# An encoder trunk in float32 on one core: earlier norms, tables loaded under the output product, a weight limit of six, values one step later

## The chip, the cores and the metric

The kernel runs on one core of a Trainium2 chip. A core has five engines that take their instructions in order, each from its own queue: TensorE (PE, matrix products), VectorE (DVE), ScalarE (ACT), GpSimd (POOL) and SyncE (SP, which here only issues transfers). Transfers (DMAs) run beside them; the kernel issues them from SP, POOL and ACT. The metric is the time of one execution on the device in microseconds (us); lower is better.

## The reference

Two layers act on `x` (512 tokens, 1024 wide); each also reads 256 memory tokens. All is float32.

```python
for i in range(DEPTH):                       # 2
    h = rmsnorm(x, norm_g[i])
    mem_h = rmsnorm(mem, mem_norm_g[i])
    if i % 2 == 0:                           # layer 0: 8 heads x 3 dilation groups
        proj = einsum('bsd,de->bse', h, w_in_a[j])
        o_mix = mixer_dilated(qkv, qn_a[j], kn_a[j], ang_a)
    else:                                    # layer 1: 8 query heads, 2 key/value heads
        proj = einsum('bsd,de->bse', h, w_in_b[j])
        o_mix = mixer_axial_gqa(q, k, v, qn_b[j], kn_b[j], ang_b)
    o_mem = memory_attention(q_mem, mem_h, w_mem_kv[i], ...)      # 4 heads
    y = concatenate([o_mix, o_mem]) * silu(gate)
    x = x + einsum('bse,ed->bsd', y, w_out[i])
```

## The kernel before

**Products.** A float32 product is made of three products of a rounded type: every operand is split into a high half (a cast on ACT) and a low half (the difference, on DVE), and PE adds high x high, high x low and low x high (`mm3`, lines 163 to 166). For weights the cast is line 287 (tile `wh`) and the difference line 297 (tile `wo`).

**Blocks.** Most projections take seven quarter products instead of eight (Strassen's scheme as Winograd wrote it; `s_chunk`). A block is such a group of seven. Their left sides are sums and differences of quarters of the activations (`S1` to `S4`), their right sides the weight quarters "21", "11", "22" and the sums T1 to T4, which are formed by accumulating transfers: for layer 1's blocks T1 by line 252, T2 by 261, T3 by 266, T4 by 271, all issued on POOL. T2 is added from the finished T1, T4 from the finished T2. In `s_chunk` a PSUM bank is copied out by ACT (`keep`, line 364, tile `sn`) before a later product adds to the same bank.

**Order.** The program is written out slot by slot. After each unit of matmuls (some 24 small or 12 large ones) the code calls `drv.free()`, then `W.advance()`, which moves the weights one step, then `drv.tick()`, which runs one step of every waiting generator: the `urgent` ones, then the `bulk` ones (attention), then what was handed to `drv.late`. A `yield n` in a generator means: go on n slots later. What is issued in a tick stands in the engines' queues behind what came earlier in the code, and in order.

**Weights.** `W.dma` (line 229) loads pieces of 512 KB into a ring of 23 tiles of 4 KB a partition (`m4`), as long as the number of loaded pieces not yet split is below `KEEP` of the next piece's kind: T2b are the memory weights of layer 1, O1 the pieces of the output product that go without the seven-product scheme, W1b the seven blocks of layer 1's input projection that have one unit a product. `W.sum` issues the accumulating transfers two steps after the load; `W.hi` and `W.lo` do the two halves, up to four pieces ahead.

**The start.** `mem_kv` makes the memory's keys and values of layer 0; between its units `ahead` finishes the memory's norm (`norm_2`, `norm_3`) and `prep` (spawned for slot 2) norms x in four blocks: `norm_1` (two squares on ACT with their sums, then POOL), `norm_2` (two products on DVE, line 469), then transposes and splits (`first_t`, `diffs_t`, `rest_t`).

**Layer 0's end.** `attn_a` handles a head in some twenty steps. `scale` multiplies the exponentials by `c`, eight instructions on DVE (line 1157). `gates` multiplies the heads by the gate; in the last gate block (g is 2) the product (line 781), its cast on ACT (784) and the low half (786) stand in three steps. `out_proj` then makes the output product: one seven-product block, and `out_rest`, two plain products of four slots each. Behind it in the code come the rotary tables of layer 1: three loads (lines 1254 to 1259) and five DVE instructions (`setup_b`, lines 1262 to 1265).

**Layer 1's attention.** `attn_b` is a pipeline of 32 items (8 heads, 4 blocks of 128 queries). In one bulk step it scores item t, takes the exponentials of t-1, scales t-2, transposes t-3 (`turn`, line 1388; halves in `hi`, `lo`, lines 1392 and 1397) and multiplies t-4 by the values (`pv`, into tile `ob`). Every second `pv` makes a half of a head; a full head goes to memory (`odb`) and is loaded back by the gate (`og`, line 763).

Of the kernel before, what the change touches and what calls it, by code (L numbers as in the profile page):

```python
# [10 lines left out]
F32 = mybir.dt.float32  # L11
# [10 lines left out]
TCKW = {}  # L22
NBIG, NM4, NS2, SCRATCH = 7, 23, 13, 2048
RING, LEAD = 4, 2
BULK, ACTIVE, SET_AT, WARM, MEM_B, PREP_Y, ACC_AT, PREP_B, HALF, SET_B = 2, 2, 15, 1, 12, 1, 4, 1, {"a": 3, "b": 3, "o": 0}, 1
MEM_STEP = 1, 1
MEM_D = 4
PD = 2
# [7 lines left out]

SEQ = [1, 2, 0] + list(range(3, len(PLAN)))
T1_DMA = 17
KEEP = {"T2": 8, "T2b": 4, "O1": 4, "W1": 9, "W2": 10, "W2s": 9, "W1b": 7, "W2b": 9}


class Driver:
# [83 lines left out]
def trunk_kernel(ctx: ExitStack, tc: tile.TileContext, x, mem, wall, norm_g, mem_norm_g, gcol,  # L126
# [408 lines left out]
    def rest_t(H, c, ds):  # L535

        def put(k, f):
            hi, lo = slot(H, k, c)
            A.copy(hi, f)
            drv.late(lambda: V.tensor_tensor(lo, f, hi.bitcast(F32), ALU.subtract))  # L540

        cs = slice(c * 128, (c + 1) * 128)
        s1, s2_, s4, s3, f22 = [full[k][:, :, cs] for k in ("S1", "11", "12", "S3", "22")]
        V.tensor_tensor(s2_, s1, s2_, ALU.subtract)
        V.tensor_tensor(s4, s4, s2_, ALU.add)
        put("S2", s2_)
        yield ds[0]
        put("S4", s4)
        yield ds[1]
        put("S3", s3)  # L550
        yield ds[2]
        put("22", f22)
        yield 1
# [193 lines left out]
    def gates(od, o_done):  # L747
# [3 lines left out]
        def gate(H, first, g, half=False):  # L751


            yt = [[m4(F32R, "y").rearrange("p (h t) -> p h t", h=2) for _ in range(2)] for _ in range(2)] if g == 2 else None
            if g < 2:
                yf[g] = [m4(name="yf") for _ in range(2)]

            def ev(q, u, t):
                i, j = int(q[0]) - 1, int(q[1]) - 1
                h0, ts = first + 2 * j, slice(i * 256, (i + 1) * 256)  # L760
                def load():
                    o = s2(name="og")
                    nc.sync.dma_start(o.rearrange("p (h t) -> p h t", h=2), od[h0:h0 + 2, :, ts].rearrange("h p t -> p h t"))
# [17 lines left out]
                V.tensor_tensor(t, t, o, ALU.mult)  # L781
                yield 1
                tv = t.rearrange("p (h t) -> p h t", h=2)
                A.copy(yt[j][0][:, :, ts], tv)
                yield 1
                V.tensor_tensor(yt[j][1][:, :, ts], tv, yt[j][0][:, :, ts].bitcast(F32), ALU.subtract)
# [54 lines left out]

        return gate, prep_y, YW, ys

    def out_proj(YW, ys, src, evac, tiles, half=False):

        acc, done = {}, set()

# [14 lines left out]

        drv.spawn(load(), ACC_AT)
        s_chunk(512, YW, ev, half=half)
        out_rest(ys, acc, done, evac)


# [22 lines left out]
        if c % 2:  # L890
            W.dma(2)
    H, H2 = {}, {}
    xb = [halves(t) for t in xt]

    def prep():

        n = {}
        for c in range(5):
            if c < 4:
                n[c] = norm_1(xb[c])  # L900
            if c:
# [156 lines left out]
    def attn_a(h, qk0, qs, ks, v12, n_done):  # L1058
# [95 lines left out]
        def scale(o):  # L1154
            for b in range(4):
                c0, c1 = (64 if o == 0 and b == 0 else 0), (192 if o == 0 and b == 3 else 256)
                V.tensor_scalar(prob[o][:, b, c0:c1], prob[o][:, b, c0:c1], c[:, o, b:b + 1], 0.5, ALU.mult, ALU.mult)

        def turn(o):

# [85 lines left out]
                yield EO[2]  # L1246
                yield from rest_t(H2, b - 2, EO[3:])

    drv.spawn(mem_norm(1), MEM_B)
    out_proj(YW, ys, xv, ev_o, lambda: [m4(name="acc") for _ in range(2)])  # L1250

    ropeB = pool.tile([128, 2048], F32, tag="tabs", name="tabs", bufs=1).rearrange("p (a c b e) -> p a c b e", a=2, c=2, b=4)
    tb_raw = s2(name="tbraw").rearrange("p (c b e) -> p c b e", c=2, b=4)
    nc.sync.dma_start(tb_raw, tab_b.rearrange("p (c b e) -> p c b e", c=2, b=4))
    grB = s2(name="grB")[:, 0:256].rearrange("p (a e) -> p a e", a=2)
    nc.sync.dma_start(grB[:, 0], qn_b.to_broadcast([128, 128]))
    nc.sync.dma_start(grB[:, 1], kn_b.to_broadcast([128, 128]))

    def setup_b():
        V.tensor_scalar(grB[:, 0], grB[:, 0], QS, None, ALU.mult)
        for qk in range(2):
            for cs_ in range(2):
                V.tensor_tensor(ropeB[:, qk, cs_].rearrange("p b (h e) -> p b h e", h=2),
                                tb_raw[:, cs_, :, None, :].to_broadcast([128, 4, 2, 64]),
                                grB[:, qk].rearrange("p (h e) -> p h e", h=2)[:, None].to_broadcast([128, 4, 2, 64]), ALU.mult)
# [45 lines left out]
    def rope_b(t, qk, i, d):  # L1313
# [5 lines left out]
        V.tensor_tensor(v(ta), v(t), ropeB[:, qk, 0, 2 * i:2 * i + 2, None, :].to_broadcast([128, 2, 2, 128]), ALU.mult)  # L1319
        V.tensor_tensor(v(sb), v(t), ropeB[:, qk, 1, 2 * i:2 * i + 2, None, :].to_broadcast([128, 2, 2, 128]), ALU.mult)  # L1320
# [35 lines left out]
    def attn_b():  # L1356
# [51 lines left out]
        def out_(i):  # L1408
# [147 lines left out]
```

## Time and profile before

| | us |
|---|---|
| median of 3 runs | 972.17 |
| lowest, highest | 968.25, 972.54 |
| profiled execution, its own time | 966.39 |
| its span, first to last instruction | 964.6 |
| PE busy | 947.5 (98%) |
| DVE busy | 790.6 (82%) |
| ACT busy | 683.0 (71%) |
| POOL busy | 339.7 (35%) |
| granted TensorE clock, mean | 0.998 |

The profile is one execution, told by hardware. "L297" is line 297 of the kernel. A wait reads "who line <- who released it: us in total, times, longest". A row of a timeline has start, length, engine, line, operation, output<-inputs, size and count, and in brackets the idle time before it and what ended it. A window has busy time per engine, the granted clock, the share of the 16 DMA engines and GB/s. PEld is the loading of PE's fixed operand, which overlaps the matmuls.

### The profile page before, as it was taken

What the parts mean: (1) busy time and instruction counts of PE and PEld (TensorE: products, weight loads), DVE (VectorE), ACT (ScalarE), POOL (GpSimd) and SP (SyncE); (2) the same over time, 40 slices, a digit from 0 to 9 for tenths busy, and PEclk for the clock granted to TensorE, in tenths of its full rate; (3) what the DMA queues carried; (4) which work ended last, traced back from release to release, by engine and by line L of the source; (5) the groups of instructions that cost most, each with busy time, mean ns of one, the idle gap of its engine ahead of it and who ended that gap; (6) DMA issues with size and microseconds to landing.
All of it is one profiled execution on the core that took longest, in us unless ns stands there. A gap on an engine that the chain in (4) does not pass through costs nothing.

```text
span 964.6 us, 16613 instructions
## 1 busy us (share of the span) xinstructions
PE 947.5 (98%) x5682; PEld 833.3 (86%) x5682; DVE 790.6 (82%) x1411; ACT 683.0 (71%) x1701; POOL 339.7 (35%) x482
## 2 busy tenths in 40 slices
PE   8999999999999999999999999999899999999998
PEld 5879888888888888888899997888899999998876
DVE  4898676888888888888797999879888997779873
ACT  5874689686868686868675767556778887878760
POOL 1512523556454545464726011323233231011011
PEclk9999999999999999999999999999999999999999
DMA  9799946869686868685858989969976696877744
GB/s 361 234 285 341 288 112 177 288 123 265 147 259 151 258 155 261 154 262 132 269 147 216 276 194 281 310 198 308 284 174 148 175 239 163 222 202 173 191 144 131
DMA packets 89130, 209.81 MB, mean 218 GB/s; under 512 B 25299, under 2 KB 36051, under 8 KB 89045
## 3 DMA queue, kind: packets, MB, share of 16 engines
q1 hardware_dynamic: 69892, 145.76, 43.6%
q0 software_dynamic: 17856, 60.83, 33.7%
q10 hardware_dynamic: 1296, 2.16, 0.6%
q8 instruction: 45, 0.74, 0.3%
q14 instruction: 41, 0.33, 0.1%
HBM read 157.27 MB, written 12.65 MB: 176 GB/s over the span
## 4 chain that ended last, share of the span: by engine, by line
PE 86%; DVE 8%; ACT 3%; DMA 2%; issue 1%; SPq 0%; DVEq 0%; ACTq 0%
PE pj L166 22%; PE pj L164 22%; PE pj L165 22%; DVE wo L297 3%; PE qT L571 2%; PE sa L1089 1%; PE oo L1191 1%; PE pt L1170 1%; PE sa L1085 1%; PE ptb L1388 1%; DMA og<-odb 1%; PE xT L475 1%; PE ob L165 1%; PE row L592 1%; PE ob L166 1%
## 5 line engine op out<-in xcount | busy, mean ns | idle before, releaser
L297 DVE TENSOR_TENSOR wo<-wl,wh 128x1024 fp32r<-128x1024 f32 x255 | 314.2, 1238 | 5.8 <-ACT wh L287 5.7
L287 ACT CAST wh<-wl 128x1024 fp32r<-128x1024 f32 x255 | 269.2, 1059 | 55.9 <-PE pj L166 33.7
L164 PE MATMUL pj<-wh,hS 128*128 128x512 f32 (+1 forms) x448 | 164.3, 367 | 0.0
L165 PE MATMUL pj<-wo,hS 128*128 128x512 f32 (+1 forms) x448 | 158.8, 355 | 4.4 <-DVE wo L297 4.4
L166 PE MATMUL pj<-wh,hS 128*128 128x512 f32 (+1 forms) x448 | 158.7, 354 | 0.0
L164 PE MATMUL pj<-wh,h 128*128 128x512 f32 (+1 forms) x336 | 122.4, 364 | 0.0
L166 PE MATMUL pj<-wh,h 128*128 128x512 f32 (+1 forms) x336 | 118.5, 353 | 0.0
L165 PE MATMUL pj<-wo,h 128*128 128x512 f32 (+1 forms) x336 | 118.4, 352 | 0.1
L424 POOL TENSOR_TENSOR rstd<-mse,half 128x4 f32<-128x4 f32 (+2 forms) x98 | 102.2, 1043 | 8.2
L165 PEld LDWEIGHTS pj<-wo,hS 128*128 128x128 f32 x448 | 85.7, 191 | 15.3 <-DVE wo L297 5.3
L166 PEld LDWEIGHTS pj<-wh,hS 128*128 128x128 f32 x448 | 85.5, 191 | 12.2
L164 PEld LDWEIGHTS pj<-wh,hS 128*128 128x128 f32 x448 | 85.5, 191 | 10.4 <-ACT sn L364 0.4
L364 ACT COPY sn<-pj 128x512 f32<-128x512 f32 x132 | 73.9, 590 | 22.8 <-PE pj L166 19.2
L423 POOL TENSOR_SCALAR mse<-hss 128x4 f32<-128x4 f32 (+1 forms) x86 | 44.1, 513 | 124.0 <-ACT junk L559 120.2
L559 ACT ACTIVATE junk<-sn 128x128 f32<-128x128 f32 x264 | 79.0, 308 | 1.7 <-DVE sn L375 1.7
L1033 POOL TENSOR_TENSOR ta<-sn,tabs 128x128 f32<-128x128 f32 (+1 forms) x64 | 37.0, 579 | 120.0 <-DVE sn L564 91.6
L381 DVE TENSOR_TENSOR sn<-pj,sn 128x512 f32<-128x512 f32 x99 | 67.5, 684 | 5.4 <-PE pj L166 5.0
L166 PEld LDWEIGHTS pj<-wh,h 128*128 128x128 f32 x336 | 63.5, 189 | 8.9
L165 PEld LDWEIGHTS pj<-wo,h 128*128 128x128 f32 x336 | 63.7, 190 | 8.0 <-DVE wo L297 0.8
L164 PEld LDWEIGHTS pj<-wh,h 128*128 128x128 f32 x336 | 63.7, 190 | 7.2
L271 POOL DMA_DIRECT2D wl<-wl x33 | 29.1, 881 | 115.3 <-DVE wo L297 64.4
L164 PE MATMUL pj<-hS,wh 128*128 128x256 f32 x192 | 55.9, 291 | 0.0
(231 smaller groups left out, 2464.3 us busy)
## 6 DMA issues: line engine op xcount, KB each, us to landing
wl<-in_wall_dram SPq DMA_DIRECT2D x222, 512.0 KB, 7.0
wl<-wl POOLq DMA_DIRECT2D x66, 512.0 KB, 6.2
wl<-in_wall_dram POOLq DMA_DIRECT2D x42, 512.0 KB, 8.4
acc<-sn POOLq DMA_DIRECT2D x16, 256.0 KB, 5.2
od<-o SPq DMA_DIRECT2D x12, 256.0 KB, 5.8
og<-od SPq DMA_DIRECT2D x12, 256.0 KB, 6.8
odb<-o SPq DMA_DIRECT2D x12, 256.0 KB, 3.0
og<-odb SPq DMA_DIRECT2D x12, 256.0 KB, 4.5
```

The costliest lines, as they stand in the source:

```text
L164: T.matmul(o, lh, rh, start=start, stop=False, skip_group_check=True)
L165: T.matmul(o, lh, rl, start=False, stop=False, skip_group_check=True)
L166: T.matmul(o, ll, rh, start=False, stop=stop, skip_group_check=True)
L271: G.dma_start(self.tile[key], self.tile[c, "T2", x], accum_op=ALU.add)
L287: A.copy(wh, self.tile[self.items[i]])
L297: V.tensor_tensor(wo, self.tile[key], wh.bitcast(F32), ALU.subtract)
L364: A.copy(t, b)
L381: V.tensor_tensor(t, b, t, ALU.subtract if q == "12" else ALU.add)
L423: G.tensor_scalar(e, ss, EPS, None, ALU.add)
L424: G.tensor_tensor(r, e, half[:, 0:n], ALU.pow)
L559: A.activation(jk, p[:, j * 128:(j + 1) * 128], AF.Square, scale=QS, accum_out=ss[:, j:j + 1])
L1033: G.tensor_tensor(ta[:, 0:n], xn[:, 0:n, 0:32], ropeA[:, 0, b, s0:s0 + n], ALU.mult)
```

## The change

Seven edits, none of which changes what is computed:

1. `norm_1` of x's first block moves from `prep` into `ahead`; `prep` then starts with `norm_2` of that block, and each of its steps is one slot earlier.
2. In `rest_t` the sum that makes S4 moves behind the first wait, next to S4's own split. This holds for both layers.
3. `setup_b` takes in the tile and the loads of the tables, waits three slots, and then does its products; it is spawned between the block and `out_rest` of layer 0's output product (`side`).
4. `KEEP`: T2b and O1 from 4 to 6, W1b from 7 to 6.
5. In the last gate block the cast follows its product in the same slot (`drv.late`), and a step is gone.
6. The factor 0.5 moves into `c`; head 7 is scaled on ACT instead of DVE.
7. In `attn_b`, `pv` and `out_` go from step 4 to step 5.

```diff
-BULK, ACTIVE, ..., SET_B = 2, 2, 15, 1, 12, 1, 4, 1, {"a": 3, "b": 3, "o": 0}, 1
+BULK, ACTIVE, ..., SET_B = 2, 2, 15, 1, 12, 1, 4, 1, {"a": 3, "b": 3, "o": 0}, 3
...
-KEEP = {"T2": 8, "T2b": 4, "O1": 4, "W1": 9, "W2": 10, "W2s": 9, "W1b": 7, "W2b": 9}
+KEEP = {"T2": 8, "T2b": 6, "O1": 6, "W1": 9, "W2": 10, "W2s": 9, "W1b": 6, "W2b": 9}
...
         V.tensor_tensor(s2_, s1, s2_, ALU.subtract)
-        V.tensor_tensor(s4, s4, s2_, ALU.add)
         put("S2", s2_)
         yield ds[0]
+        V.tensor_tensor(s4, s4, s2_, ALU.add)
         put("S4", s4)
...
                 V.tensor_tensor(t, t, o, ALU.mult)
-                yield 1
                 tv = t.rearrange("p (h t) -> p h t", h=2)
-                A.copy(yt[j][0][:, :, ts], tv)
+                drv.late(lambda: A.copy(yt[j][0][:, :, ts], tv))
                 yield 1
...
-    def out_proj(YW, ys, src, evac, tiles, half=False):
+    def out_proj(YW, ys, src, evac, tiles, half=False, side=None):
...
         s_chunk(512, YW, ev, half=half)
+        if side:
+            drv.spawn(side())
         out_rest(ys, acc, done, evac)
...
-    xb = [halves(t) for t in xt]
+    xb, nx = [halves(t) for t in xt], {}
     def prep():
-        n = {}
-        for c in range(5):
+        for c in range(1, 5):
             if c < 4:
-                n[c] = norm_1(xb[c])
-            if c:
-                norm_2(xb[c - 1], n[c - 1], rows["x"])
+                nx[c] = norm_1(xb[c])
+            norm_2(xb[c - 1], nx[c - 1], rows["x"])
             if 1 < c < 4:
                 first_t(H, xb[c - 2], c - 2)
             yield 1
...
             for j in range(2):
                 A.copy(rows["x"][j], gain[j])
+            nx[0] = norm_1(xb[0])
             norm_3(mb[1], M, 128, 0)
...
-        V.tensor_tensor(c.rearrange("p o b -> p (o b)"), e[:, 0], rd, ALU.mult)
+        V.scalar_tensor_tensor(c.rearrange("p o b -> p (o b)"), e[:, 0], 0.5, rd, ALU.mult, ALU.mult)
...
-                V.tensor_scalar(prob[o][:, b, c0:c1], prob[o][:, b, c0:c1], c[:, o, b:b + 1], 0.5, ALU.mult, ALU.mult)
+                if h == 7:
+                    A.activation(prob[o][:, b, c0:c1], prob[o][:, b, c0:c1], AF.Copy, scale=c[:, o, b:b + 1])
+                else:
+                    V.tensor_scalar(prob[o][:, b, c0:c1], prob[o][:, b, c0:c1], c[:, o, b:b + 1], None, ALU.mult)
...
     def setup_b():
+        ropeB.append(pool.tile([128, 2048], F32, tag="tabs", ...))
+        tb_raw = s2(name="tbraw")...
+        nc.sync.dma_start(tb_raw, tab_b...)
+        grB = s2(name="grB")...
+        nc.sync.dma_start(grB[:, 0], qn_b...)
+        nc.sync.dma_start(grB[:, 1], kn_b...)
+        yield SET_B
         V.tensor_scalar(grB[:, 0], grB[:, 0], QS, None, ALU.mult)
...
-    drv.spawn(setup_b(), SET_B)
...
+    out_proj(YW, ys, xv, ev_o, lambda: [m4(name="acc") for _ in range(2)], side=setup_b)
...
-        yield from pipeline(32, (0, score, 0), (4, pv, 0), (3, turn, 0), (2, scale, 0), (1, exps, 0),
-                            (0, top, 1), (1, recip, 1), (3, hi, 1), (3, lo, 1), (4, out_, 1),
+        yield from pipeline(32, (0, score, 0), (5, pv, 0), (3, turn, 0), (2, scale, 0), (1, exps, 0),
+                            (0, top, 1), (1, recip, 1), (3, hi, 1), (3, lo, 1), (5, out_, 1),
```

More of the change, by code (lines that the diff above doesn't have):

```diff
@@ L24 @@
 RING, LEAD = 4, 2
-BULK, ACTIVE, SET_AT, WARM, MEM_B, PREP_Y, ACC_AT, PREP_B, HALF, SET_B = 2, 2, 15, 1, 12, 1, 4, 1, {"a": 3, "b": 3, "o": 0}, 1
+BULK, ACTIVE, SET_AT, WARM, MEM_B, PREP_Y, ACC_AT, PREP_B, HALF, SET_B = 2, 2, 15, 1, 12, 1, 4, 1, {"a": 3, "b": 3, "o": 0}, 3
 MEM_STEP = 1, 1
@@ L1247, in ev_o @@
                 yield from rest_t(H2, b - 2, EO[3:])
[L1249 to L1259, printed above, removed]
-    def setup_b():
+    ropeB = []
+    def setup_b():
+        ropeB.append(pool.tile([128, 2048], F32, tag="tabs", name="tabs", bufs=1).rearrange("p (a c b e) -> p a c b e", a=2, c=2, b=4))
+        tb_raw = s2(name="tbraw").rearrange("p (c b e) -> p c b e", c=2, b=4)
+        nc.sync.dma_start(tb_raw, tab_b.rearrange("p (c b e) -> p c b e", c=2, b=4))
+        grB = s2(name="grB")[:, 0:256].rearrange("p (a e) -> p a e", a=2)
+        nc.sync.dma_start(grB[:, 0], qn_b.to_broadcast([128, 128]))
+        nc.sync.dma_start(grB[:, 1], kn_b.to_broadcast([128, 128]))
+        yield SET_B
         V.tensor_scalar(grB[:, 0], grB[:, 0], QS, None, ALU.mult)
@@ L1264, in setup_b @@
             for cs_ in range(2):
-                V.tensor_tensor(ropeB[:, qk, cs_].rearrange("p b (h e) -> p b h e", h=2),
+                V.tensor_tensor(ropeB[0][:, qk, cs_].rearrange("p b (h e) -> p b h e", h=2),
                                 tb_raw[:, cs_, :, None, :].to_broadcast([128, 4, 2, 64]),
@@ L1268, in setup_b @@
                 yield 1
-    drv.spawn(setup_b(), SET_B)
+    drv.spawn(mem_norm(1), MEM_B)
+    out_proj(YW, ys, xv, ev_o, lambda: [m4(name="acc") for _ in range(2)], side=setup_b)
     od_b = dram.tile([12, 128, S], F32, name="odb", bufs=1)
@@ L1318, in rope_b @@
         ta, sb = s2(name="ta"), s2(name="sb")
-        V.tensor_tensor(v(ta), v(t), ropeB[:, qk, 0, 2 * i:2 * i + 2, None, :].to_broadcast([128, 2, 2, 128]), ALU.mult)
-        V.tensor_tensor(v(sb), v(t), ropeB[:, qk, 1, 2 * i:2 * i + 2, None, :].to_broadcast([128, 2, 2, 128]), ALU.mult)
+        V.tensor_tensor(v(ta), v(t), ropeB[0][:, qk, 0, 2 * i:2 * i + 2, None, :].to_broadcast([128, 2, 2, 128]), ALU.mult)
+        V.tensor_tensor(v(sb), v(t), ropeB[0][:, qk, 1, 2 * i:2 * i + 2, None, :].to_broadcast([128, 2, 2, 128]), ALU.mult)
         yield d[1]
```

## The prediction

> **What bounds the kernel now.** I read, in this order: the busy times of the page, the waits of PE, then windows around the places of these waits, and there the timelines of the single engines.
>
> ```profile
> PE 947.5 (98%) x5682; PEld 833.3 (86%) x5682; DVE 790.6 (82%) x1411; ACT 683.0 (71%) x1701; POOL 339.7 (35%) x482
> ...
> PE pj L165 <- DVE wo L297: 5.0, 4, 2.9
> ...
> PE ob L165 <- DVE pbT L1397: 2.2, 2, 1.4
> PE pj L166 <- DVE y L786: 1.0, 1, 1.0
> ...
> PE pj L164 <- DVE sn L381: 0.4, 1, 0.4
> ```
>
> TensorE (PE) is the bound. An edit elsewhere can only give back PE's waits, or add to them. After the start they are 8.6 us (5.0 + 2.2 + 1.0 + 0.4), in eight waits; the largest is 2.9. Most end on VectorE (DVE), by a low half of a weight (wo, L297). The windows say where:
>
> ```profile
> core 0: us, PE busy (x) PEld busy (x) DVE busy (x) ACT busy (x) POOL busy (x), PEclk, DMA share, GB/s
> 30.00:62.00 32.00, 30.36 (x146) 23.90 (x144) 30.06 (x39) 24.04 (x49) 11.51 (x15) 1.00 0.81 217
> 575.00:605.00 30.00, 28.78 (x138) 22.66 (x137) 29.16 (x52) 20.04 (x32) 4.32 (x5) 1.00 0.98 280
> 643.00:680.00 37.00, 34.15 (x196) 29.67 (x195) 33.34 (x46) 28.39 (x61) 13.36 (x18) 0.99 0.98 313
> ```
>
> In these three DVE is busy 94%, 97% and 90% of the time: PE waits there for a queue that is full.
>
> **The change part by part.** Terms are against the profiled execution's own time, 966.39 us (span 964.6).
>
> *1. x's norms one step sooner, S4's sum two steps later (start).* No work is added. The squares of x's first block move to ACT's idle time before the second transposes, and every step of `prep` is one slot earlier. But the tick of slot 2 is written ahead of the next unit's `ahead`, so x's first product with its norm now stands on DVE before the two subtractions for which PE waits:
>
> ```profile
> 22.44 1.29 DVE L161 TENSOR_TENSOR act<-xT,act 128x512 fp32r<-128x512 f32 x2
> 23.65 1.41 DVE L469 SCALAR_TENSOR_TENSOR x<-x,rstd,row 128x512 f32<-128x512 f32 x2
> ...
> 19.59 0.39 PE L166 MATMUL pj<-wh,act 128*128 128x512 f32 x1
> 19.82 0.39 PE L164 MATMUL pj<-wh,act 128*128 128x512 f32 x1
> ...
> 23.19 0.50 PE L166 MATMUL pj<-wh,act 128*128 128x512 f32 x1
> ...
> 56.83 0.50 PE L165 MATMUL pj<-wo,hS 128*128 128x512 f32 x1 [0.88 <-DVE wo L297]
> 60.51 0.50 PE L165 MATMUL pj<-wo,hS 128*128 128x512 f32 x1 [0.67 <-DVE wo L297]
> ```
>
> The 1.41 us go from behind the subtractions to between 22.4 and 23.8; the PE product of 23.19, which needs the first subtraction, slips by about 1.2. A row of PE lasts longer than the step to the next (0.39 against 0.23 near 19.6), so a wait costs some 0.2 more than its idle time: what can be won is 0.88 + 0.67 and twice 0.2, some 2.0. Ahead of the weight of 56.83 DVE now has more to do (x's second S2 sum and two low halves, 1.8 together), and ahead of that of 60.51 it has 0.6 less (one S4 sum). Carried through, PE loses 1.2 early, waits once and longer near 57, and not at 60. I take **+0.8**; bounds -2.0 (both waits gone, early slip made up) and +2.4 (slip kept, and the wait near 57 longer by 1.2).
>
> *2. Head 7's scaling on ACT, the last gate's cast in the same step (575 to 605).*
>
> ```profile
> 589.70 1.14 DVE L1157 TENSOR_SCALAR p<-p,c 128x256 f32<-128x256 f32 x4
> 591.36 1.22 DVE L297 TENSOR_TENSOR wo<-wl,wh 128x1024 fp32r<-128x1024 f32 x1
> 597.23 1.07 DVE L1157 TENSOR_SCALAR p<-p,c 128x192 f32<-128x192 f32 x4
> ...
> 592.62 0.50 PE L165 MATMUL pj<-wo,yS 128*128 128x512 f32 x1 [0.57 <-DVE wo L297]
> ...
> L691 ACT ACTIVATE pm<-pm,rdm x32: 494/507/530, 128.5 to 760.2; 128x256 f32<-128x256 f32 x32
> ```
>
> DVE loses 1.05 us ahead of the weight of 591.36 and 1.0 more at 597. The waits behind are 0.57 (wo) and 0.4 (sn), with 0.2 for each 1.4; some 0.6 lies in delays too short to be listed as waits, an estimate from PE's 28.78 of 30. ACT gains eight scalings; the nearest row is L691 at 0.5 each (0.4 apart), so 3.2 us in two groups. ACT is busy 20.04 of 30 there, and the cast behind the first group belongs to a weight of two slots later. If that cover were gone, a late snapshot of PSUM (L364) would hold PE up by up to 2. The cast of y waits on ACT for its product as before, and the low half comes a slot sooner, where its 0.6 takes back part of the gain. **-1.7**; bounds -2.0 and +0.5. For heads 0 to 6 the 0.5 moves into `c` (L1148): same instruction counts, no PE waits there, nothing.
>
> *3. Tables under the output product; six weights in flight (605 to 700).*
>
> ```profile
> 659.66 0.68 DVE L1265 TENSOR_TENSOR tabs<-tbraw,grB 128x512 f32<-128x512 f32 x1
> ...
> 675.20 0.69 DVE L545 TENSOR_TENSOR f<-f,f 128x512 f32<-128x512 f32 x1
> ...
> 677.53 2.35 DVE L297 TENSOR_TENSOR wo<-wl,wh 128x1024 fp32r<-128x1024 f32 x2
> ...
> 678.80 0.39 PE L165 MATMUL pj<-wo,hS 128*128 128x256 f32 x1 [2.85 <-DVE wo L297]
> ...
> 679.89 0.21 PE pj L164
> ...
> 684.03 0.12 PE pj L164
> ```
>
> Of the four table products, one (0.6) lies in the unbroken DVE queue before the weight of 677.53; the others had idle time behind them. They and the three loads go under the output product, where DVE and SP have room; SP takes the loads earlier, not between this layer's weights. S4's sum (L545, 0.6) goes behind the weight. So the wait of 2.85 falls by 1.2. Behind it come matmuls at half speed (0.21 apart, later 0.12), 16 of them from 679.3 to 682.7: another 1.5, which may go too. That is -1.2 to -2.7, and at most -4.4 if the wait vanished.
>
> Against it stands the limit of 7 that becomes 6. I counted the rule of `W.dma` slot by slot. The extra loads for the output and memory weights come two to four slots sooner, where PE doesn't wait for weights. But of layer 1's first block T1 is now loaded at step 186, not 184, so its accumulating transfer is issued at 188, the place of T2's until now; T2's goes to 190, behind it T4's. These are in order on POOL, and each needs the landing of the one before:
>
> ```profile
> 654.02 0.94 POOL L252 DMA_DIRECT2D wl<-in_wall_dram  x1
> ...
> 662.96 0.93 POOL L261 DMA_DIRECT2D wl<-wl  x1
> ...
> 671.78 0.87 POOL L271 DMA_DIRECT2D wl<-wl  x1 [6.97 <-DVE fS L531]
> ...
> DMA to landing us min/median/max: 8.3/10.2/12.1
> ...
> DMA to landing us min/median/max: 6.4/7.3/8.2
> ...
> DMA to landing us min/median/max: 5.5/7.3/9.0
> ...
> 683.35 0.59 ACT L364 COPY sn<-pj 128x512 f32<-128x512 f32 x1 [2.53 <-PE pj L166]
> 683.83 1.06 ACT L287 CAST wh<-wl 128x1024 fp32r<-128x1024 f32 x1
> ...
> 687.00 0.57 ACT L364 COPY sn<-pj 128x512 f32<-128x512 f32 x1
> ```
>
> The three rows of landings are those of L252 (T1), L261 (T2) and L271 (T4) between 650 and 700, two transfers each; the first of each group is the longer one but for T1 (8.3). Today T4 lands at 671.78 + 9.0 = 680.8, and ACT's cast asks at 683.83: 3.0 to spare. After, T1 starts at 662.96 and lands at 671, T2 at about 679, T4 at 687 (three times 8). Behind that cast ACT has the snapshot that stands at 687.00, and the sixth product (step 197) may not start before it; it would be done 3.8 after T4's landing (687.57 less 683.83), at 690.8. Today the third product ends at 683.35, where ACT's snapshot was released, and two steps of 24 matmuls at 0.12 lead to 689.1 for the sixth. So this place could end 1.7 later instead of 2.7 sooner. With shorter transfers (the smallest is 5.5) it would be hidden. I take **+1.3**; bounds -4.4 and +5.7 (one transfer of 12). Behind T4 on POOL stand the second block's T1 and the norms of the memory queries (L423, L424), which the attention needs some slots later. Later blocks take 4 us a slot beside attention and have slots to spare.
>
> By the Trainium skill (DMA: Bandwidth & Descriptors, Anatomy of one DMA) such a transfer takes 2.0 us and its bytes at 436 GB/s, an estimate of 3.2 for 512 KB. Then T4 would land near 675, the term would be -2.7, and the time that of the faster rival below. The rows here, 5.5 to 12.1 with the DMA share at 0.98, say otherwise.
>
> *4. Values a step later in layer 1's attention.* `pv` now finds its transposed probabilities two steps after their transposes. The two waits on pbT, 2.2 in all, 2.6 with 0.2 for each, lose their cause. If ACT was the late one, DVE's queue would be met a slot on. PE's other work there never waits today. **-2.4**; bounds -2.9 and 0. The pair of tiles is held one step longer, two of 23 such buffers.
>
> *5. The end.* The same step makes the last head's output 2.75 us later (one slot).
>
> ```profile
> 931.90 0.99 SPq L763 DMA_DIRECT2D og<-odb  x2
> ...
> 936.05 1.36 DVE L781 TENSOR_TENSOR sn<-sn,og 128x512 f32<-128x512 f32 x2 [4.06 <-DMA og<-odb]
> ...
> 938.46 1.28 DVE L375 TENSOR_TENSOR sn<-sn 128x512 f32<-128x512 f32 x2
> 939.67 1.29 DVE L786 TENSOR_TENSOR y<-sn,y 128x512 fp32r<-128x512 f32 x2
> ```
>
> og would land near 938.8, the two products end at 940.1, casts follow at once (the step saved), and L375 stands between: the low half comes at about 941.4 instead of 939.67. PE waits 1.7 longer for it. **+1.6**; bounds 0 and +2.7.
>
> Sum: 0.8 - 1.7 + 1.3 - 2.4 + 1.6 = -0.4, so 966.0 against 966.39 for the profiled execution. The median of the runs is 972.17, 5.8 above it; less 0.4 that is 971.8.
>
> **Rivals.** *Faster, the covers hold.* T4 lands before ACT asks, and the end loses little: 0 - 1.9 - 2.7 - 2.7 + 0.8 = -6.5, so 965.7. For it: every step removes DVE work just ahead of a weight for which PE waits; with one transfer fewer in flight the links may take 6 to 7. Against: DMA share 0.98. *Slower, POOL's chain.* At layer 1's first block the links take 9 to 12 rather than 8, T4 lands at 691, the snapshot ends at 694.8, +5.7; PE's idle time passes 3 us and brings the slow matmuls again, +1.5; the second block starts some 2 late behind it on POOL. With the other terms (0.8 - 1.7 - 2.4 + 1.6 = -1.7) that is +7.5, or 979.7. It decides from a landing of T4 after about 688.4 (then +4.9). For it: a transfer of L252 in this stretch took 12.1. Against: fewer loads compete. *The change doesn't do what it says:* the limit of 6 loads fewer weights ahead in seven of the blocks; the moved norm only trades one wait for another; then parts 1 and 3 give 0 and the rest -2.5, 969.7, inside the forecast.
>
> **How the numbers follow.** Forecast (971.8, own range 968 to 976): 0.48 with the rival that does nothing; faster 0.32; slower 0.20. The parts are independent, each 1 to 3 wide, about 3 together, and the median moves by some 2: 964 to 978.5 leaves out 2 in 10. About 0.5%, 4.9 us, is what a measurement of this kernel can tell from no change: faster 0.32, same 0.46, slower 0.22 (a little of the forecast's upper end).
>
> **What would show it.** Part 1: L469 ahead of L161 on DVE near 22, one PE wait near 57. Part 2: L1157 only 56 times, no PE wait on wo at 591. Part 3: L252 near 663 rather than 654, L271 near 679, ACT's cast at 684 waiting on a DMA; the wait of 2.85 smaller. Part 4: no PE wait on pbT. Part 5: L781 waits for og near 939 and PE longer for y. Wrong if L271 lands before 684, or if a wait of over 2 us shows up beside these.

## The result, and the profile after

The changed kernel took 983.78 us (median of 6 runs, 981.74 to 986.87) against 970.23 us for the kernel before on the same chip (6 runs, 968.09 to 974.64): a ratio of 1.014, with a 95% interval of 1.0111 to 1.017. It is slower by about 13.6 us; the forecast was 971.8, with a range up to 978.5. The profiled execution took 983.70 us, with a span of 981.9 where it had been 964.6.

The page of the kernel after gives the busy times, and the view of PE's waits, from 15 us on (who, on whom: us in total, times, longest), says what became of them:

```profile
PE 952.4 (97%) x5682; PEld 836.5 (85%) x5682; DVE 788.2 (80%) x1403; ACT 684.8 (70%) x1709; POOL 341.3 (35%) x482
```

```profile
PE pj L165 <- DVE wo L297: 4.5, 4, 2.6
PE pj L164 <- ACT hS L539: 4.1, 1, 4.1
PE ptb L1391 <- DVE pbT L1400: 3.6, 5, 1.3
PE qT L571 <- DVE fS L532: 2.0, 1, 2.0
PE pj L164 <- ACT wh L287: 1.9, 1, 1.9
...
PE pj L166 <- DVE act L161: 1.1, 1, 1.1
...
```

DVE became a little less busy, as meant, and PE waits more: four new waits of 2 to 4 us in total stand beside those on the low halves (wo), and by this view two of them end on ACT.

Where the time went is read by counting PE's matmuls. Each profile has 5682 of them, and the edits move matmuls by a slot at most, so the time from one matmul's start to a later one's can be compared between kernels. The stages are named by their times in the kernel before (us); the numbers are the time of the stage less that of the kernel before.

| kernel (profiled execution) | 0-62 | 570-605 | 605-640 | 640-705 | 705-800 | 800-935 | 935-end | span |
|---|---|---|---|---|---|---|---|---|
| after | +3.1 | +1.2 | +0.4 | +6.4 | +2.7 | +3.4 | +0.1 | 981.9 |
| w1b_six | -1.3 | 0.0 | +1.1 | +4.6 | +3.6 | +2.1 | +0.2 | 974.9 |
| w1b_six_pv | -0.9 | +2.5 | +0.2 | +6.4 | 0.0 | +3.0 | +0.4 | 976.3 |
| norm_sooner | +2.1 | 0.0 | +1.5 | -0.6 | 0.0 | +3.1 | -0.1 | 970.7 |
| s4_later | 0.0 | -0.1 | +1.1 | +2.5 | 0.0 | +3.5 | -0.1 | 972.0 |
| head7_act | -1.2 | -1.6 | +0.9 | +1.6 | 0.0 | +2.8 | +0.7 | 967.9 |
| cast_sooner | -1.3 | +1.7 | +0.3 | 0.0 | 0.0 | +4.0 | -1.1 | 968.1 |
| tables_under | -0.8 | -0.1 | +0.1 | +1.8 | 0.0 | +0.9 | 0.0 | 966.6 |
| extra_early | -0.1 | -0.1 | +1.6 | -0.6 | 0.0 | +3.6 | -1.3 | 967.7 |
| harmless_four | -1.3 | -1.3 | +1.6 | +4.2 | 0.0 | +1.7 | -0.8 | 969.1 |
| after_seven | +1.9 | +1.1 | +1.1 | +4.1 | 0.0 | +4.0 | +0.3 | 977.1 |
| seven_s4_back | +2.8 | +1.2 | +0.9 | +1.1 | 0.0 | +3.7 | +0.1 | 974.4 |
| values_room | -0.4 | -0.1 | +1.0 | -0.6 | +1.4 | -0.9 | +1.1 | 966.1 |
| values_room_less | -0.2 | +0.3 | +1.2 | -0.6 | 0.0 | -1.4 | +2.5 | 966.4 |
| room_h7 | -0.6 | -0.9 | -0.2 | 0.0 | 0.0 | -1.1 | +0.8 | 962.5 |
| room_h7_tables | -0.8 | +1.1 | +1.7 | +1.9 | 0.0 | +3.3 | +0.4 | 972.4 |

(62 to 570 differs by at most 0.5 in all of them and is left out.) How much of a number is scatter is seen where a kernel does not differ from before: the eight kernels without the later values step lose 0.9 to 4.0 more from 800 to 935, up to 1.6 from 605 to 640, and w1b_six_pv lost 2.5 from 570 to 605 with no edit there. So the profile of before was a lucky one between 800 and 935, by about 3; its 966.39 us against medians of 968.0 to 970.2 say the same. Four of the eight have 3.4 us of half clock somewhere from 877 to 915, and it has none. From 640 to 705 head7_act loses 1.6 with no edit there, and w1b_six and w1b_six_pv, whose edits there are the same, have 4.6 and 6.4. From 0 to 62 the kernels with no edit there take 0.1 to 1.3 less.

In the first row three places make the result: the first block of layer 1 (640 to 705) with a later one of the same kind (705 to 800), layer 1's attention (800 to 935), and the start.

**The first block.** Windows of the kernel after (busy us of each engine, then the granted clock, the DMA share and GB/s), and its timeline there:

```profile
682.60:686.00 3.40, 2.65 (x12) 2.65 (x13) 1.96 (x3) 0.00 (x0) 0.00 (x0) 0.50 1.07 219
686.00:690.00 4.00, 2.62 (x13) 2.33 (x11) 1.86 (x3) 3.00 (x4) 1.77 (x2) 0.50 0.79 155
690.00:693.00 3.00, 0.30 (x1) 0.33 (x2) 2.32 (x4) 2.39 (x4) 0.00 (x0) 0.50 1.04 176
693.00:696.30 3.30, 3.30 (x17) 3.30 (x17) 3.30 (x5) 3.30 (x12) 0.00 (x0) 0.51 0.94 286
```

```profile
668.38 0.93 POOL L252 DMA_DIRECT2D wl<-in_wall_dram  x1
...
679.40 0.87 POOL L261 DMA_DIRECT2D wl<-wl  x1 [10.09 <-DVE f L544]
...
687.19 0.87 POOL L271 DMA_DIRECT2D wl<-wl  x1 [6.00 <-DMA wl<-wl]
...
678.80 1.06 ACT L287 CAST wh<-wl 128x1024 fp32r<-128x1024 f32 x1 [2.36 <-DMA wl<-in_wall_dram]
...
686.54 1.05 ACT L287 CAST wh<-wl 128x1024 fp32r<-128x1024 f32 x1 [5.10 <-DMA wl<-wl]
...
690.61 0.62 ACT L539 CAST hS<-f 128x512 fp32r<-128x512 f32 x1 [1.07 <-DVE f L547]
...
691.26 0.69 DVE L540 TENSOR_TENSOR hS<-f,hS 128x512 fp32r<-128x512 f32 x1 [0.68 <-ACT hS L539]
691.87 0.68 DVE L381 TENSOR_TENSOR sn<-pj,sn 128x512 f32<-128x512 f32 x1
...
692.70 0.55 PE L164 MATMUL pj<-wh,hS 128*128 128x256 f32 x1 [4.07 <-ACT hS L539]
```

T2's and T4's sums are issued 0.7 after the landing of the one before: T1 lands 10.35 after its issue, at 678.73, and T2 7.12 after its own, at 686.52. (The bracket names DVE's L544 for T2's; the landing fits here, and in the kernel before and w1b_six too, where it comes 0.6 ahead of T2's issue.) ACT's casts of T1 and T2 stand at the head of its queue until the data land, 2.36 and 5.10 us, and everything behind them waits with them, the snapshot too (L364, at 688.01). PE's wait of 4.07 is for the addition L381, which needs this snapshot: PE goes on 0.15 after its end (692.55), as in all ten profiles in which PE waits at this matmul. The cast of 692.08, which the bracket names, only ended last; in w1b_six that cast ended after PE had gone on. L381 is later still in the change, because DVE first has S4's low half (L540), whose cast (690.61) waited for S4's sum (L547). Meanwhile the clock is at half from 682.6 to 696.3, 13.7 us.

### The profile page after: what moved, and what is told of

Its sections match the earlier page's. It is cut to its first block, busy times and chain, and to the rows that moved or that the text cites. A ratio compares the mean times of both kernels' runs of the same rounds, so it can differ in the third digit from the quotient of the medians.

```text
span 981.9 us, 16622 instructions
## 1 busy us (share of the span) xinstructions
PE 952.4 (97%) x5682; PEld 836.5 (85%) x5682; DVE 788.2 (80%) x1403; ACT 684.8 (70%) x1709; POOL 341.3 (35%) x482
## 5 line engine op out<-in xcount | busy, mean ns | idle before, releaser
L424 POOL TENSOR_TENSOR rstd<-mse,half 128x4 f32<-128x4 f32 (+2 forms) x98 | 104.6, 1067 | 8.2
L164 PEld LDWEIGHTS pj<-wh,hS 128*128 128x128 f32 x448 | 86.6, 193 | 14.5 <-issue 4.3
L166 PEld LDWEIGHTS pj<-wh,hS 128*128 128x128 f32 x448 | 86.6, 193 | 12.2
L364 ACT COPY sn<-pj 128x512 f32<-128x512 f32 x132 | 73.4, 589 | 14.9 <-PE pj L166 14.7
L381 DVE TENSOR_TENSOR sn<-pj,sn 128x512 f32<-128x512 f32 x99 | 67.7, 685 | 6.3 <-PE pj L166 5.8
L271 POOL DMA_DIRECT2D wl<-wl x33 | 29.3, 889 | 105.6 <-DVE wo L297 47.4
L261 POOL DMA_DIRECT2D wl<-wl x33 | 31.1, 978 | 81.8 <-ACT sn L364 16.5
```

Of the source, the lines that this page charges most:

```text
L164: T.matmul(o, lh, rh, start=start, stop=False, skip_group_check=True)
L166: T.matmul(o, ll, rh, start=False, stop=stop, skip_group_check=True)
L261: G.dma_start(self.tile[key], self.tile[c, "T1", x], accum_op=ALU.add)
L364: A.copy(t, b)
L381: V.tensor_tensor(t, b, t, ALU.subtract if q == "12" else ALU.add)
L424: G.tensor_tensor(r, e, half[:, 0:n], ALU.pow)
```

## The experiments

The kernels below are the one before with some of the seven edits, if nothing else is said. Ratios are against runs of the kernel before on the same chip, with 95% intervals.

### The limit of six alone

```diff
-"W1b": 7
+"W1b": 6
```

> The kernel before with one edit: at most six weights of layer 1's input projection in flight instead of seven. Theory (the limit starts T1 of the first block a slot late, POOL's chain T1, T2 cannot catch up, ACT's queue stands at the cast of T2): PE loses about 6 us more than before between 670 and 700, with a wait of 3 to 4 us on ACT and the clock at half behind it, T1's sum issued near 663 to 668 instead of 654, and some 2 us near 790 by the same chain at a later block: 976 to 979. Rival (the tables and the sooner loads of the output and memory weights crowd the transfers; the limit alone is hidden): within 1.5 us of before, about 970.

Measured: 975.65 us against 968.04, a ratio of 1.0072 (1.0051 to 1.0093). The timeline of this kernel, POOL's sums and then ACT's casts:

```profile
662.69 0.94 POOL L252 DMA_DIRECT2D wl<-in_wall_dram  x1
...
673.56 0.87 POOL L261 DMA_DIRECT2D wl<-wl  x1 [9.93 <-DVE hS L540]
...
681.71 0.87 POOL L271 DMA_DIRECT2D wl<-wl  x1 [6.36 <-DMA wl<-wl]
```

```profile
673.05 1.05 ACT L287 CAST wh<-wl 128x1024 fp32r<-128x1024 f32 x1
...
681.07 1.04 ACT L287 CAST wh<-wl 128x1024 fp32r<-128x1024 f32 x1 [4.32 <-DMA wl<-wl]
682.02 0.61 ACT L539 CAST hS<-f 128x512 fp32r<-128x512 f32 x1
682.54 0.58 ACT L364 COPY sn<-pj 128x512 f32<-128x512 f32 x1
...
688.63 1.05 ACT L287 CAST wh<-wl 128x1024 fp32r<-128x1024 f32 x1 [2.09 <-DMA wl<-wl]
```

T1's sum is issued at 662.69, where the prediction had put it (662.96), and T2's cast waits until 681.07, where before it ran near 673.9 right behind T1's. Behind it the snapshot L364 comes at 682.54, and PE waits 3.1 for what DVE makes of it. The stage loses 4.6, and a later block 3.6 more, where ACT's cast stands 6.64 for such a sum; w1b_six_pv, with the same limit, does not have this second loss. The limit costs time by itself; the rival falls.

### The limit of six and the values a step later

```diff
-"W1b": 7
+"W1b": 6
...
-(4, pv, 0) ... (4, out_, 1)
+(5, pv, 0) ... (5, out_, 1)
```

> The limit of six and the values one step later, nothing else. My forecast for the later step was -2.4 against the same kernel without it, the two waits on the transposed probabilities gone. The theory now: a pair of tiles is held one step longer, the ring of 23 tiles is full, the next pair gets tiles which the product of the values is still reading, so ACT's cast waits for PE and PE's next transposes wait for the low half: about +3 against the limit of six alone, 979 to 982, with about five waits of PE at the transposes, 3 to 4 us together, after 800.

Measured: 979.09 against 968.04, 1.0107 (1.007 to 1.0143). PE's waits of this kernel from 800 to 935:

```profile
PE ptb L1388 <- DVE pbT L1397: 3.3, 4, 1.3
...
```

The two waits of `ob` on pbT are gone, as the prediction had it; four others have come, of the transposes `ptb`. The step gains nothing here: +3.0 from 800 to 935, as in the kernels without it (+0.9 to +4.0). In the whole time the loss of some 3 against the limit of six alone is there: all four runs (978.09 to 981.49) are above all nine of w1b_six (973.04 to 977.10). The two profiles differ by 1.4 only, and not in this stage alone, so they do not show how much of the 3 is the ring's. The kernel after has the mechanism in three rows of its timeline:

```profile
851.66 0.59 ACT L1395 CAST pbT<-ptb 128x512 fp32r<-128x512 f32 x1 [3.85 <-PE ob L165]
...
852.28 0.69 DVE L1400 TENSOR_TENSOR pbT<-ptb,pbT 128x512 fp32r<-128x512 f32 x1 [3.73 <-ACT pbT L1395]
...
853.03 0.66 PE L1391 MATMUL ptb<-ident,pb 128*128 128x128 f32 x4 [1.29 <-DVE pbT L1400]
```

The cast of a new pair of tiles does not wait for its own transposes, which ended near 848, but for the product of the values, `ob`, that reads the old pair. So the new pair got the old pair's place in the ring of 23, and PE's next transposes wait for the low half of a cast which waited for PE.

### The values a step later, with room in the ring

```diff
-(4, pv, 0) ... (4, out_, 1)
+(5, pv, 0) ... (5, out_, 1)
...
-"W2b": 9}
+"W2b": 7}
...
-self.live < KEEP[kind]
+self.live < {26: 5}.get(block, KEEP[kind])               # values_room_less
+self.live < {24: 6, 25: 5, 26: 5}.get(block, KEEP[kind]) # values_room
```

> The values one step later, with room made for them at that place only: the limit is seven up to block 23, six in block 24, five in blocks 25 and 26, and seven instead of nine for the last block's pieces. Theory (the ring of 23 tiles is full where the attention runs, and the new pair of tiles waits for the old one): the waits of PE at the transposes between 800 and 870, 5 us with the run of six and the later step, shrink to under 1; what the later step gains after 870 (3 to 4 us against typical runs of before) stays: 965 to 968. Rival (the waits at the transposes come from DVE and ACT being late, whatever the ring holds): they stay, 970 to 974. A third way: the lower limits delay the sums on POOL, with waits on a weight near 800 to 860.

> The same with less room: seven up to block 25, five in block 26, seven for the last block. By the ring theory the wait near 810 stays (0.9), those from 845 on go: 966 to 969. By the rival the same waits as without room, 970 to 974.

Measured: values_room_less 967.08 against 969.01, 0.998 (0.9968 to 0.9992), so a little faster than before; values_room 969.71, 1.0018 (0.9993 to 1.0042), no difference. PE's waits of values_room_less from 800 to 935:

```profile
PE ptb L1388 <- ACT pb L1379: 0.5, 1, 0.5
PE ptb L1388 <- DVE pbT L1397: 0.2, 1, 0.2
```

With two pieces fewer in flight at the end, the 3.3 became 0.2, and the stage is 1.4 shorter than in the profile of before, some 4 shorter than in the other kernels. DVE and ACT have the same work as in w1b_six_pv, so the ring was the cause. That the wait near 810 would stay was wrong. With still fewer in flight the third way of the expectation shows: values_room lost 1.4 just before 800 and 1.4 more from 800 to 810.

### The start: x's norms a slot sooner

```diff
+            nx[0] = norm_1(xb[0])
             norm_3(mb[1], M, 128, 0)
...
-        for c in range(5):
+        for c in range(1, 5):
```

> The kernel before with x's norms one slot sooner, nothing else. Theory: PE loses 3 us more than before in the first 62 us (1.1 at the product whose left side stands behind the norm on DVE, 2 at the transposes of a block whose product with the norm is not done): 973. Rival (the two waits of 0.88 and 0.67 on the low halves near 57 and 60 fall away with it, which was my sum): +0.8, 971.

Measured: 972.05 against 968.04, 1.0029 (1.0009 to 1.005). PE's waits of this kernel from 15 to 62, and DVE's timeline around the largest:

```profile
PE qT L571 <- DVE fS L532: 2.0, 1, 2.0
PE pj L166 <- DVE act L161: 1.1, 1, 1.1
PE pj L165 <- DVE wo L297: 0.9, 1, 0.9
```

```profile
41.88 2.35 DVE L297 TENSOR_TENSOR wo<-wl,wh 128x1024 fp32r<-128x1024 f32 x2
44.15 0.68 DVE L531 TENSOR_TENSOR fS<-xT,f 128x512 f32<-128x512 f32 x1
44.75 0.67 DVE L532 TENSOR_TENSOR fS<-f,xT 128x512 f32<-128x512 f32 x1
```

The 1.1 is the slip that the prediction worked out as 1.2, and one of the two waits near 57 and 60 is gone. The wait of 2.0 is not in it. The differences S1 and S3 (L531, L532) read the transposed x out of PSUM; a slot sooner they are issued right behind two low halves (2.35), and PE's transposes of the memory's keys, which come next, need one of the same four PSUM tiles (tag `at`). In the kernel before the instruction that reads these transposes (L620) stands on DVE ahead of the differences. The clock then goes to half, in this kernel for 3.4 us from 45.8 on; the kernel after has it at 47.7:

```profile
47.70:51.20 3.50, 3.50 (x10) 2.73 (x9) 2.49 (x4) 3.50 (x6) 0.86 (x1) 0.51 1.06 305
```

### S4's sum later

```diff
-        V.tensor_tensor(s4, s4, s2_, ALU.add)
         put("S2", s2_)
         yield ds[0]
+        V.tensor_tensor(s4, s4, s2_, ALU.add)
         put("S4", s4)
```

> The kernel before with S4's sum behind the first wait, nothing else. My sum gave -0.6 of DVE ahead of the low half near 677, so a smaller wait there. Theory now, from the trace of the harmless four: the sum lands on DVE behind two low halves (2.35 together), S4's cast stands on ACT for it, and behind that cast the snapshot and the weights' casts come some 4 us later: +2.5 to +4.2 between 668 and 705, 970 to 973. Rival (the four together crowd the transfers): within 1 us of before.

Measured: 974.62 (4 runs) against 968.25, 1.0064 (1.0045 to 1.0084). Its timeline, DVE and then ACT:

```profile
679.32 2.35 DVE L297 TENSOR_TENSOR wo<-wl,wh 128x1024 fp32r<-128x1024 f32 x2
...
682.25 0.68 DVE L547 TENSOR_TENSOR f<-f,f 128x512 f32<-128x512 f32 x1
```

```profile
682.97 0.62 ACT L539 CAST hS<-f 128x512 fp32r<-128x512 f32 x1 [4.28 <-DVE f L547]
683.49 0.58 ACT L364 COPY sn<-pj 128x512 f32<-128x512 f32 x1
683.97 1.05 ACT L287 CAST wh<-wl 128x1024 fp32r<-128x1024 f32 x1
```

The sum (L547 here) is behind the two low halves, and ACT's cast of S4 stands 4.28 us for it with the snapshot and the casts of the weights behind it. PE then waits 1.17 for the addition L381, as in the change. This stage loses 2.5 in the profile, of which head7_act has 1.6 without this edit. That the whole loses 6 is not explained by this stage: from 800 on the profile has +3.4 of the scatter told above, and the rest is not settled.

### Head 7 on ACT; the last cast sooner

```diff
# head7_act
+                if h == 7:
+                    A.activation(prob[o][:, b, c0:c1], prob[o][:, b, c0:c1], AF.Copy, scale=c[:, o, b:b + 1])
# cast_sooner
-                yield 1
...
-                A.copy(yt[j][0][:, :, ts], tv)
+                drv.late(lambda: A.copy(yt[j][0][:, :, ts], tv))
```

> The kernel before with the factor in the coefficients and head 7 scaled on ACT, nothing else. My sum with the sooner cast was -1.7, from the waits of 0.57 on the low half near 592 and 0.4 on the copy near 597. Rival (ACT's eight scalings stand ahead of casts and copies for which DVE and PE wait): +0.5 to +1.5 between 575 and 605. The whole time cannot tell these apart; the waits of PE between 575 and 605 can.

> The kernel before with the last gate block's cast in the slot of its product, nothing else. Expected: 0 between 575 and 605 by both theories there; at layer 0's last product block one slot less of delay, at most 0.5 us less or more between 605 and 640; the time is that of before within 1 us.

Measured: head7_act 969.31 against 968.77, 0.9998 (0.9977 to 1.002); cast_sooner 971.22, 1.0027 (1.0008 to 1.0047). From 575 to 612, head7_act has this wait left of the two near 592 and 594, and cast_sooner these rows on DVE:

```profile
PE pj L164 <- DVE sn L381: 0.3, 1, 0.3
```

```profile
575.54 0.69 DVE L785 TENSOR_TENSOR y<-sn,y 128x512 fp32r<-128x512 f32 x1
...
577.52 1.22 DVE L297 TENSOR_TENSOR wo<-wl,wh 128x1024 fp32r<-128x1024 f32 x1
...
593.92 0.68 DVE L785 TENSOR_TENSOR y<-sn,y 128x512 fp32r<-128x512 f32 x1
594.53 0.68 DVE L381 TENSOR_TENSOR sn<-pj,sn 128x512 f32<-128x512 f32 x1
```

Head 7's scaling takes away the wait on the low half, and ACT has the room. Its stage is 0.9 to 1.6 shorter in three profiles (head7_act, harmless_four, room_h7) and 1.1 longer in a fourth (room_h7_tables); in the whole time the gain is lost in the scatter. The sooner cast brings the low half of y (L785) a slot sooner too, and it now stands ahead of a weight's low half near 577 and of the addition L381 near 594, for both of which PE waits. The order is shown; its size in the profile (+1.7) is within what kernels without the edit lost there (up to 2.5), and the ten runs say 0.27%.

### The tables; the limit of six for memory and output weights; the four together

```diff
# tables_under
+    out_proj(YW, ys, xv, ev_o, lambda: [m4(name="acc") for _ in range(2)], side=setup_b)
# extra_early
-"T2b": 4, "O1": 4
+"T2b": 6, "O1": 6
# harmless_four: both of these, head 7 on ACT and S4's sum later
```

> The kernel before with one edit: the tables' loads and products beneath the output product. My sum gave about -1.2 to -2.7, from a smaller wait on the low half near 677 (2.85 before) and fewer matmuls at half speed behind it. Rival (the loads and the DVE products meet the residual stream's own work there, and POOL's sums land later): 0 to +3 between 605 and 705, 968 to 971.

> The kernel before with the limit for the memory weights of layer 1 and the plain pieces of the output product at six instead of four. My sum gave nothing. Theory now, from the run with seven weights again, where the first block of layer 1 still lost 4 us more than before and T2's transfer took 10.9 us where it had taken 8.2: if the sooner loads crowd these sums, this run loses 2 to 4 us between 668 and 705, 970 to 972; if the loads are harmless it is within 1 us of before.

> The four edits which alone changed nothing or were not run alone: head 7 on ACT, S4's sum later, tables beneath the output product, the limit of six for memory and output weights. If the parts add up: 967 to 969, within 0.3% of before, with the first block of layer 1 (668 to 705) at most 2 us over before. Rival (together they crowd the transfers for the first block, which would explain the 4 us that the run with seven weights again kept there): +3 to +4 there, 971 to 973.

Measured: tables_under 968.61 against 968.77, 0.9997 (0.998 to 1.0015); extra_early 968.87, 0.9991 (0.9973 to 1.0009); harmless_four 970.87 against 969.01, 1.0024 (1.0013 to 1.0035). The first two change nothing in the whole time: the wait near 677 did not shrink with the tables out of the way (3.8 in that profile). The four lose 4.2 in the first block, 2.4 more than the tables alone; s4_later names the part, by the addition L381, for which PE waits 1.97 here. But the four together lose less (0.24%) than S4's sum alone (0.64%), so the size of this part in the whole time is open.

### Taking parts back; what is left

```diff
# after_seven: the kernel after, and
-self.live < KEEP[kind]
+self.live < KEEP[kind] + (20 <= block < 26)
# seven_s4_back: after_seven with S4's sum where it was before
# room_h7: values_room_less and head 7 on ACT
# room_h7_tables: room_h7, the tables, the limit of six for memory and output weights
```

> The changed kernel, with seven weights in flight again for the first six of the seven blocks of layer 1's input projection. Theory: the chain on POOL starts as early as before, the wait of 4.1 on ACT near 688, the half-speed matmuls behind it and the wait of 1.9 near 797 go, 7 to 8 us less than the changed kernel: 975 to 977. Rival (the loads of the tables and the extra loads ahead of layer 1 delay the chain, not the limit): at most 2 us less, 982.

> The changed kernel with two parts taken back: seven weights up to block 25, and S4's sum where it was. Theory (limit and S4's sum are two causes of one wait, either alone is enough): the first block of layer 1 loses at most 2 us over before, where it lost 6.4 with both and 4.1 with the limit alone taken back; 976 to 978 in all, since the norm, the sooner cast and the full ring stay. Rival: it stays at 4, 979 to 980.

> The values a step later with five weights in block 26 and seven pieces in the last block, and head 7 on ACT. If the gains add up: 1.6 less between 575 and 605, 965 to 967; if head 7's gain is taken back at layer 1's first block, as in the run of that part alone (+1.6 there), the same as without it, 967.

> The same with the tables beneath the output product and the limit of six for memory and output weights: all of the change but the norm, S4's sum, the sooner cast and the limit of six where it costs. If these parts are without effect also together: 965 to 967. If they crowd T1's and T2's transfers: +2 to +4 between 668 and 705, 968 to 970.

Measured: after_seven 980.31 against 968.04, 1.0125 (1.0082 to 1.0167); seven_s4_back 975.63 against 968.25, 1.0075 (1.0047 to 1.0103); room_h7 966.34, 0.9975 (0.9961 to 0.9989); room_h7_tables 969.44, 1.0017 (1.0002 to 1.0032).

The limit alone taken back left 4.1 of the 6.4 in the first block, against my theory; the limit and S4's sum taken back left 1.1. So S4's sum is worth 3.0 there, and the limit, which cost 4.6 alone, 2.3 on top of the rest. The two are two holds on ACT's one queue, and while ACT stands for one, part of its standing for the other is hidden. The queue's order shows that this can be; the sizes are of one profile each, in a stage with a scatter of about 2. What seven_s4_back still loses is the start, the sooner cast and the ring, whose waits at the transposes are there (3.2), though its +3.7 from 800 to 935 is no more than the scatter.

room_h7 is faster than the kernel before by 0.25%, the lowest ratio of all, though its interval overlaps with that of values_room_less; head 7 and the later values step with room are all that it takes from the change. From 800 to 935 PE has two waits in it, 0.8 and 0.2.

With the tables and the sooner loads besides, the gain is gone, though each of these two alone costs nothing. Why is open: its profile, of the slowest of its ten runs (974.3), loses in four stages at once, about as the scatter does.

## Why the prediction was wrong

*Step 1, the start: +0.8, measured +2.1 alone and +3.1 within the change.* The slip of 1.2 came (1.1), and the wait at 60 went. The step that failed is "every step of `prep` is one slot earlier", costed through the low halves alone. The differences out of PSUM were moved too, past two low halves of a weight, and the PSUM bank that they release was not looked at.

*Step 2: -1.7, measured -1.6 for head 7 and +1.7 for the cast, +1.2 within the change.* For head 7 the mechanism was right (the wait near 592 is gone), and the size as far as four profiles of -1.6 to +1.1 tell. Its 0.6 for short delays does not come out of the row named for it: of 30 less 28.78, 1.22, the two waits are 0.97, which leaves 0.25. The eight scalings on ACT took 0.49 us (median) where 0.5 was taken. For the cast the sentence "its 0.6 takes back part of the gain" had the mechanism and not the size: PE waits at two places behind it, not at one.

*Step 3: +1.3, measured +6.4 and +2.7.* The failed step is that the chain was tested at its last link only. The prediction has T2 landing at 679, but never asks when ACT wants it. In the kernel before, the casts of T1 and T2 are this row of ACT's timeline:

```profile
672.94 1.99 ACT L287 CAST wh<-wl 128x1024 fp32r<-128x1024 f32 x2
```

The second of the two starts near 673.9 (half of 1.99 later). So 5 us of standing still (679 less 673.9) were in the numbers; ACT waited 4.32 with the limit alone and 5.10 in the change. T4, on which the sum looked, decided little: its cast waited 2.09 with the limit alone, and in the change not at all. The rival named the chain, its place and its sign, and put 5.7 + 1.5 + 2 = 9.2 on it, where 9.1 was measured in these two stages, S4's part included; it was given 0.20. That the two numbers agree is luck: its 5.7 came from T4's landing too, and its 2 was for the second block, while the 2.7 arose in a later one. The second failed step is "S4's sum (L545, 0.6) goes behind the weight. So the wait of 2.85 falls by 1.2". PE's wait on that weight hardly moved (2.65), while ACT's cast of S4 waits for the sum, and behind that cast ACT has the snapshot and the weights.

By the Trainium skill (DMA: Bandwidth & Descriptors, Anatomy of one DMA: about 2.0 us and the bytes at 436 GB/s) 512 KB would take an estimate of 3.2 us. In the rows of the change T1's sum took 10.4 from its issue at 668.38 to the cast at 678.80, T2's 7.1 (679.40 to 686.54), with the DMA share at 0.79 to 1.07. The trace does not agree here; the rows of before that the prediction used, 5.5 to 12.1, hold for these two, while T4's took 4.6.

*Step 4: -2.4, measured +3.4 against a profile that was lucky there by about 3.* The failed step is "The pair of tiles is held one step longer, two of 23 such buffers": the ring was named, not counted, and its being full was put at nothing. The waits on pbT that were to go went; 3.6 of waits at the transposes came in their place. With room in the ring the same comparison gives -1.4 (values_room_less), so the term has the right sign there.

*Step 5: +1.6, measured +0.1.* The last rows of the change:

```profile
951.85 0.89 SPq L763 DMA_DIRECT2D og<-odb  x2
...
954.50 1.36 DVE L781 TENSOR_TENSOR sn<-sn,og 128x512 f32<-128x512 f32 x2 [1.55 <-DMA og<-odb]
...
955.78 1.28 DVE L375 TENSOR_TENSOR sn<-sn 128x512 f32<-128x512 f32 x2
...
956.98 1.29 DVE L785 TENSOR_TENSOR y<-sn,y 128x512 fp32r<-128x512 f32 x2
```

The load is issued 20.0 later than before, of which 17.2 is the delay of everything: 2.75 was predicted. But it lands 2.65 after its issue (954.50 less 951.85) where it took 4.15 before, and the three DVE instructions follow each other, where a weight's low half of 1.22 (937.33, between L781 and L375) stood among them before: the low half comes 17.3 after that of before (956.98 less 939.67). The term's size failed, because the transfer's time and DVE's queue were taken as fixed.

Together the terms were -0.4, the profile has +17.3 (981.9 less 964.6), the medians +13.6. Of the 17.3, 9.1 are in step 3's stages, 3.4 in step 4's and 3.1 in the start.

## What to carry to other kernels

When a chain of transfers moves, set each link's landing against the moment at which its own consumer asks, and ask what stands behind that consumer in its in-order queue; the last link is not the one that must decide. An instruction that is moved "behind" a long one on its engine holds up every engine whose next instruction needs it, and two holds on one queue can hide each other when parts are tried one at a time. A buffer that is held a step longer is free only if the ring has one to spare: a cast that waits for the reader of the previous tile, rather than for its own input, is how a full ring looks in a trace.

## What the hardware showed that was not expected

A wait of PE of 2.0 us (start) or 2.65 us (first block) was enough for half the clock. It lasts 3.4 us before (679.2 to 682.6), as long in the change at the start (the window at 47.7), and 13.7 in the change from 682.6 to 696.3, with one wait of 4.07 within: four times 3.4. Besides the waits it costs some 3.3: 37 matmuls ran 0.21 apart in place of 0.12. The Trainium skill (TensorE: Matmul & The Clock Gate, The HAM clock gate) has a free-running window of about 3.4 us, and half rate after an idle window: the lengths agree, while in these rows a window in which PE was idle for 2 us was enough.

The length of a wait alone does not decide. In every profile with more than one half-rate stretch they start whole multiples of 3.413 us apart (in the change at 47.7, 682.6 and 983.0: 186 and 88 of them). The wait of 2.85 near 677 lies within one such step before, and half rate follows. In values_room, as in three other profiles, a wait as long at the same place falls into two steps, and none follows (the first two rows are of before, the others of values_room):

```profile
675.80:679.20 3.40, 0.55 (x5) 0.40 (x4) 3.02 (x5) 3.40 (x7) 0.00 (x0) 1.00 1.05 269
679.20:682.60 3.40, 3.40 (x18) 3.40 (x18) 3.40 (x6) 1.61 (x3) 0.00 (x0) 0.51 1.07 277
674.90:678.30 3.40, 1.60 (x14) 1.39 (x12) 2.99 (x6) 3.38 (x6) 1.75 (x2) 1.00 1.03 325
678.30:681.70 3.40, 2.35 (x19) 2.35 (x20) 3.40 (x5) 3.07 (x5) 0.00 (x0) 1.00 1.07 318
```

So where a wait falls decides over a loss of some 1.5 (16 matmuls in 679.2 to 682.6), and this is a part of the scatter between profiles.

The time of a sum of 512 KB on POOL varies, and no run here shows with what: T2's of the first block, from its issue to the cast of T2 that it released, took 11.1 in s4_later (664.98 to 676.04) and 7.5 in w1b_six (673.56 to 681.07). In seven of the fourteen profiles with a limit of seven in this block T2 landed 10.9 to 11.7 after its issue, and in just these PE waited 3.16 to 3.97 for T1's low half; in the other seven, 7.9 to 10.3, it waited 2.84 to 2.86. head7_act and tables_under are among the first, which goes with their +1.6 and +1.8 there.
